# Retention's transposes moved behind the next values, two units of modulation sums moved back, 14 idle products added

## The chip, the cores and the metric

The kernel runs on one core of a Trainium2 chip. The metric is the device time of one execution in microseconds (us); lower is better. TensorE (PE in the profile) multiplies, VectorE (DVE) and ScalarE (ACT) work on elements, GpSimd (POOL) does a few small things, and SyncE (SP) issues nearly all loads, in order, on one queue.

## What is computed

The program is two transformer blocks in float32 on 256 tokens of width 1024. Only the first half of the first block matters here:

```
mod = silu(c) @ w_ada + b_ada                 # 6 x 1024: shift, scale, gate for both halves
h = modulate(rms_norm(x, norm1_g), sh1, sc1)
proj = h @ w_in                               # 14336 columns: retention, attention, two gates
ro = group_norm(retention(rotary(q), rotary(k), v))       # 4 heads, values of 512
ret_out = (silu(rg) * ro) @ w_ret_out
att_out = dilated_attention(3 groups of 4 heads) @ w_att_out
merged = sigmoid(gate_a) * ret_out + sigmoid(gate_b) * att_out
x = x + g1 * (merged @ w_o)
```

`g1` and the modulation of the second half (`sh2`, `sc2`, `g2`) are not needed before `w_o`, though they come from the same vector `c`.

## The kernel before

**Products.** Every float32 product is three products of a rounded type: an operand is split into a high part and a remainder, and `mm3` (L169 to L171) adds high x high, high x low, low x high. Activations are kept transposed (channels on partitions, `h1T`) as such pairs. Weights come in 512 KB loads `raw` (L130, all on SP's queue, a ring of 6); ScalarE rounds a load to `whi` (L145), VectorE subtracts to `wlo` (L148), and both live in rings of 6. A projection of 512 columns is 96 products of 128x256 (or 48 of 128x512 where tokens are the rows).

**Order.** Except where the code says `manual_schedule`, a list scheduler orders the instructions of each engine by its own model of costs; each engine and each queue then works in that order, and an instruction that waits holds up all that stand behind it.

**Start** (ordered by hand). Five steps of `START` each finish the modulation of one or two blocks of 128 channels and use them for the first queries, keys and values. `ada_cols` loads the columns of `w_ada` in pieces (`araw`), VectorE multiplies and sums them row by row (L394, L396), PE adds over partitions (L414, L415, in `rest`), VectorE adds the bias (L417, L419), ScalarE makes `h1T` (L510, L511), PE runs the queries (12 products for one block). `rest(n)` starts with n products of zeros, `busy` (L176), 128x256 in a narrow type. `setup_rest` and constants follow.

**Retention.** For each of 4 heads h: values `a_v` (L601), scores, gate `a_g`, `ret_out` of the two heads before when there are some waiting (`late`), then o (L625 to L627), its mean and variance, the normed rows `y` (L637, VectorE), their transposes (L644, PE) into `r` (L647, ScalarE), times the gate (L648, VectorE), and the split of `r` into `rT` (L289). `ret_out` reads `rT` of two heads. In head 0 three small products of `hot` (L663) and the setup of the second block (L1022 among it) follow.

**Attention.** Three groups of four heads; for each head scores (L701, L702), sum with the bias and maximum (L704, L705, VectorE), `nmx` (L706), exponentials (L707, ScalarE), transposes (L711, PE), product with the values (L716 to L718). Then four projections of the gates (L735, L737), the three groups combined into `att` (L765, VectorE), its transposes (L771), the split into `attT` (L289), `w_att_out`, and `w_o`.

**The rest of the modulations.** Eight units are in the list `side`: the two halves of the gate row `g1` (`ada_row(0, j)`), blocks 0, 2, 4 and 6 of the second half's shift and scale (`ada_block`), the two halves of `g2`. A unit loads 2 MB of `w_ada` in four pieces of 512 KB (for blocks, each piece is two transfers of 256 KB) into buffers of their own, makes eight sums on VectorE (L394 once, L396 seven times) and ends in a product (L415 for blocks, L435 for rows) and a small VectorE operation (L417 and L419, or L436). The buffers `araw` are four during retention (`phase is pr`) and two afterwards. `SIDE[i]` says how many units are pulled after head i (0 to 3), group i - 4 (4 to 6), and the i - 7th gate projection (7 to 10); the scheduler may start what is pulled earlier than that, as buffers allow.

Of the kernel before, what the change touches and what calls it, by code (L numbers as in the profile page):

```python
# [10 lines left out]
F32 = mybir.dt.float32  # L11
# [68 lines left out]
class Kern:  # L80
# [273 lines left out]
    def first(self, done, after):  # L354
# [118 lines left out]
        with tc.manual_schedule():  # L473
# [33 lines left out]
            def activations(kb, sums):  # L507

                tmp = pr.tile([128, 256], F32, name=self.nm("ht"), tag="ht")
                S.activation(tmp, xT[:, kb, :], AF.Identity, scale=mod[:, 8 + kb : 9 + kb], bias=mod[:, kb : kb + 1])  # L510
                S.activation(hT[0][:, kb, :], tmp, AF.Copy)  # L511
                step(sums)
                V.tensor_sub(hT[1][:, kb, :], tmp, hT[0][:, kb, :])
# [15 lines left out]
            for i, g in enumerate(START):  # L529
# [9 lines left out]
                    sums, rest = ada_cols(0, n[0], len(n), 8 - ADA_PE[i + 1])  # L539
                for kb in g:  # L540
                    activations(kb, sums)
                queries(g[0], *qk, (0,))
                last = (g[0], *vs)
                if raws:
# [46 lines left out]
        for h in range(RET_H):  # L591
# [7 lines left out]
                    rotary(qk[:, 2 + j], a_k[j])  # L599
            if h:  # L600
                a_v = self.proj_nat(hT, w_in, [(2048 + h * 512, 512)])  # L601
            q, k = qk[:, h % 2], qk[:, 2 + h % 2]
            v = vcopy(a_v, pr, "v")

# [30 lines left out]
            y = pr.tile([128, 2, 512], F32, name=self.nm("y"), tag="y", bufs=1)  # L635
            for t in range(2):
                V.tensor_scalar(y[:, t], o[t], mv[:, t, 0:1], rs[:, t : t + 1], op0=OP.subtract, op1=OP.mult)  # L637
            r = pr.tile([128, 4, 256], F32, name=self.nm("r"), tag="r", bufs=1)
            for j in range(2):
                p = self.ps(128, 2, 256)  # L640
                for b in range(2):
                    blk = 2 * j + b
                    for t in range(2):
                        PE.transpose(p[:, b, t * 128 : t * 128 + 128], y[:, t, blk * 128 : blk * 128 + 128], self.ident)  # L644
                for b in range(2):
                    ch = h * 4 + 2 * j + b
                    S.activation(r[:, 2 * j + b], p[:, b], AF.Identity, bias=p1[:, 64 + ch : 65 + ch], scale=p1[:, 48 + ch : 49 + ch])  # L647
            V.tensor_mul(r, r, sg)  # L648
            o4 = (h % 2) * 4
            self.split_to(rT[0][:, o4 : o4 + 4], rT[1][:, o4 : o4 + 4], r)  # L650
            if h % 2 == 1:
                late = (rT, (h - 1) * 4)
            if h == 0:
# [14 lines left out]
                self.second_setup()  # L668
            for _ in range(SIDE[h]):
                side.pop(0)()  # L670
        ret_out(*late)
        pr_.close()

# [1322 lines left out]
G1_FREE = 0  # L1996
FREE = 8
REST = 3
SIDE = (0, 0, 0, 2, 0, 2, 1, 1, 0, 1, 1)
BUSY = (0, 7, 13, 0, 9)  # L2000
START = ((0,), (1,), (2, 3), (4, 5), (6, 7))
EARLY = 1
# [136 lines left out]
```

## Time and profile before

| | us |
|---|---|
| runs (three) | 1258.31, 1258.60, 1258.93 |
| median | 1258.6 |
| profiled execution | 1255.0 |
| its span, first to last instruction | 1253.2 |
| PE busy | 1215.2 (97%) |
| DVE busy | 953.8 (76%) |
| ACT busy | 739.3 (59%) |

Times in the rows below are microseconds from the start of the span. In a row of the timeline stand the start, the duration, engine, line of the code, operation, what is written from what, and in brackets how long the engine stood idle before and what ended that. A PE row's duration includes the pipeline's length; the time between two products is read from start to start. The granted clock (PEclk) is 1.00 at 2.4 GHz and 0.50 at 1.2 GHz.

### The profile page before, as it was taken

To read this page: it belongs to the slowest core of one execution; us is meant where nothing else is said; L and a number is where in the kernel's file an instruction comes from. 1 tells how busy PE (TensorE), PEld (TensorE's weight loads), DVE (VectorE), ACT (ScalarE), POOL (GpSimd) and SP (SyncE) were. 2 spreads that over 40 slices of the span, in tenths; PEclk is the share of its full clock that TensorE was granted. 3 is DMA by queue.
4 is the path that set the end of the run, shared out by engine and by line. 5 is a ranking of instruction groups with operands and counts; after the bars stand their busy time and mean duration, and the time that the engine had idled before them with its cause. 6 is when DMAs were issued, how large, how long until landed. Compare 5 with 4: busy or idle time off the path is not lost.

```text
span 1253.2 us, 20725 instructions
## 1 busy us (share of the span) xinstructions
PE 1215.2 (97%) x7675; PEld 1071.7 (86%) x7675; DVE 953.8 (76%) x1650; ACT 739.3 (59%) x1149; POOL 41.6 (3%) x101
## 2 busy tenths in 40 slices
PE   8999999999999999999999998999999999899995
PEld 7878988988989889998898987888879988788884
DVE  6999656574678766555589677999988967798995
ACT  4554444445554655444367663978766665588873
POOL 0010000000000000000010011000000000100000
PEclk9999999999999999999999999999999999999998
DMA  9996554796677656666473432999867342399991
GB/s 312 320 312 209 185 169 152 229 292 187 186 250 250 195 183 197 189 198 187 140 234 109 130 101 73 356 346 360 307 211 227 104 132 84 112 372 343 366 316 55
DMA packets 177170, 271.99 MB, mean 217 GB/s; under 512 B 16363, under 2 KB 109216, under 8 KB 177060
## 3 DMA queue, kind: packets, MB, share of 16 engines
q1 hardware_dynamic: 175252, 265.70, 64.4%
q10 hardware_dynamic: 1296, 3.81, 1.0%
q8 instruction: 62, 1.02, 0.3%
q0 software_dynamic: 512, 1.08, 0.2%
q14 instruction: 48, 0.39, 0.1%
HBM read 268.41 MB, written 2.12 MB: 216 GB/s over the span
## 4 chain that ended last, share of the span: by engine, by line
PE 78%; DVE 10%; DMA 4%; ACT 3%; POOL 2%; issue 2%; SPq 0%; POOLq 0%; DVEq 0%; ACTq 0%
PE ps L171 21%; PE ps L170 21%; PE ps L169 21%; DMA araw<-in_w_ada 2%; DVE wlo L148 2%; DMA raw<-in_w_in 1%; PE ps L1283 1%; PE ps L1264 1%; DVE zc L1196 1%; ACT whi L145 1%; PE ps L1681 1%; DVE ada L396 1%; PE ps L1873 1%; POOL s L285 1%; PE ps L176 1%
## 5 line engine op out<-in xcount | busy, mean ns | idle before, releaser
L145 ACT ACTIVATE whi<-raw 128x1024 fp32r<-128x1024 f32 (+3 forms) x348 | 356.3, 1039 | 262.7 <-PE ps L170 146.5
L148 DVE TENSOR_TENSOR wlo<-raw,whi 128x1024 fp32r<-128x1024 f32 x334 | 398.8, 1205 | 136.5 <-ACT whi L145 134.3
L169 PE MATMUL ps<-h1T,whi 128*128 128x256 f32 x576 | 162.9, 283 | 1.6 <-ACT h1T L511 1.6
L171 PE MATMUL ps<-h1T,wlo 128*128 128x256 f32 x576 | 162.2, 282 | 0.0
L170 PE MATMUL ps<-h1T,whi 128*128 128x256 f32 x576 | 162.0, 281 | 0.0
L148 DVE TENSOR_TENSOR wlo<-far,whi 128x1024 fp32r<-128x1024 f32 x100 | 118.3, 1220 | 7.3 <-ACT whi L145 6.8
L145 ACT ACTIVATE whi<-far 128x1024 fp32r<-128x1024 f32 x100 | 103.6, 1059 | 19.5 <-PE ps L171 18.0
L169 PEld LDWEIGHTS ps<-h1T,whi 128*128 128x128 f32 x576 | 109.0, 189 | 3.4 <-ACT h1T L511 1.7
L170 PEld LDWEIGHTS ps<-h1T,whi 128*128 128x128 f32 x576 | 109.5, 190 | 1.1 <-issue 0.5
L171 PEld LDWEIGHTS ps<-h1T,wlo 128*128 128x128 f32 x576 | 109.1, 190 | 0.2 <-issue 0.2
L169 PE MATMUL ps<-whi,xg 128*128 128x512 f32 x256 | 103.0, 402 | 0.0
L171 PE MATMUL ps<-whi,xg 128*128 128x512 f32 x256 | 100.7, 393 | 0.0
L170 PE MATMUL ps<-wlo,xg 128*128 128x512 f32 x256 | 100.6, 393 | 0.0
L396 DVE SCALAR_TENSOR_TENSOR ada<-araw,silu_c,ada 128x512 f32<-128x512 f32 (+1 forms) x88 | 62.6, 712 | 10.0 <-DMA araw<-in_w_ada 8.1
L169 PE MATMUL ps<-h2T,whi 128*128 128x256 f32 x224 | 62.0, 277 | 0.0
L170 PE MATMUL ps<-h2T,whi 128*128 128x256 f32 x224 | 62.0, 277 | 0.0
L171 PE MATMUL ps<-h2T,wlo 128*128 128x256 f32 x224 | 61.9, 276 | 0.0
L171 PEld LDWEIGHTS ps<-whi,xg 128*128 128x128 f32 x256 | 48.1, 188 | 10.4
L170 PEld LDWEIGHTS ps<-wlo,xg 128*128 128x128 f32 x256 | 48.2, 188 | 9.3 <-DVE wlo L148 0.4
L169 PEld LDWEIGHTS ps<-whi,xg 128*128 128x128 f32 x256 | 48.1, 188 | 8.8
L171 PE MATMUL ps<-whi,ffh 128*128 128x512 f32 x128 | 50.4, 394 | 0.0
L170 PE MATMUL ps<-wlo,ffh 128*128 128x512 f32 x128 | 50.2, 392 | 0.0
(517 smaller groups left out, 2888.3 us busy)
## 6 DMA issues: line engine op xcount, KB each, us to landing
raw<-in_w_in SPq DMA_DIRECT2D x124, 512.0 KB, 4.9
raw<-in_w_ff SPq DMA_DIRECT2D x64, 512.0 KB, 3.7
far<-in_w_gate SPq DMA_DIRECT2D x68, 256.0 KB, 5.2
far<-in_w_up SPq DMA_DIRECT2D x68, 256.0 KB, 5.9
araw<-in_w_ada SPq DMA_DIRECT2D x64, 256.0 KB, 4.9
far<-in_w_down SPq DMA_DIRECT2D x32, 512.0 KB, 5.9
raw<-in_w_down SPq DMA_DIRECT2D x32, 512.0 KB, 7.0
raw<-in_w_gate SPq DMA_DIRECT2D x60, 256.0 KB, 5.5
```

What stands on the lines that cost most here:

```text
L145: self.nc.scalar.activation(hv, raw, AF.Copy)
L148: self.nc.vector.tensor_sub(lv, raw, hv)
L169: mm(out, l[0], r[0], start=first, stop=False)
L170: mm(out, l[0], r[1], start=False, stop=False)
L171: return mm(out, l[1], r[0], start=False, stop=last)
L176: self.nc.tensor.matmul(p, self.idle, self.idle.unsqueeze(1).to_broadcast([128, 2, 128]), start=True, stop=True)
L285: self.nc.gpsimd.tensor_tensor(dst, t, self.mhalf[:, :w] if len(src.shape) == 2 else self.mhalf[:, :w].rearrange("p (a b) -> p a b", a=src ...
L396: V.scalar_tensor_tensor(acc, raws[k], sc[:, k : k + 1], acc, op0=OP.mult, op1=OP.add)
L1196: V.scalar_tensor_tensor(zc[:, b], xp_[:, i, k : k + 256], cw(k), zc[:, b], op0=OP.mult, op1=OP.add)
L1264: PE.matmul(p[:, t], qT[:, j, t * 128 : t * 128 + 128], kT[:, j], start=True, stop=True)
L1283: PE.matmul(p[:, t, j], PTs[j][:, s, t * 128 : t * 128 + 128], v[:, s, h * 64 : h * 64 + 64], start=j == 0 and t == 0 and s == 0, stop=j = ...
L1681: self.nc.tensor.matmul(p[kb // 2][:, kb % 2], xh[i][:, t, kb * 128 : kb * 128 + 128], P[:, t, hf * 256 : hf * 256 + 256], start=t == 0 an ...
```

## The change

Three things. (a) In the first step of the start, 14 idle products are put on PE between the end of `rest` and the queries, into the accumulator that the first query product then starts anew. (b) The part of a retention head from the transposes of `y` to the split into `rT` becomes a function `gated`, and it is called a head later, behind the next head's values; for head 3 it is called right before the last `ret_out`. (c) The table `SIDE` pulls no unit after head 3 any more, and two more units at the gates. Units keep their sequence, so each is pulled later than it was: the two rows of `g1` after group 1 and block 0 after group 2 (before: after head 3, and blocks after groups 1 and 2), blocks 2 and 4 after the first gate projection, block 6 after the second, the rows of `g2` after the third and the fourth.

```diff
@@ start, in the loop over START
                 for kb in g:
                     activations(kb, sums)
+                if i == 0:
+                    self.busy(a_q[0][:, 0].rearrange("p (a b) -> p a b", a=2), 14)
                 queries(g[0], *qk, (0,))
@@ retention, loop over heads
             if h:
                 a_v = self.proj_nat(hT, w_in, [(2048 + h * 512, 512)])
+                waiting()
             q, k = qk[:, h % 2], qk[:, 2 + h % 2]
             v = vcopy(a_v, pr, "v")
...
-            r = pr.tile([128, 4, 256], F32, name=self.nm("r"), tag="r", bufs=1)
-            for j in range(2):
-                p = self.ps(128, 2, 256)
...
-            V.tensor_mul(r, r, sg)
-            o4 = (h % 2) * 4
-            self.split_to(rT[0][:, o4 : o4 + 4], rT[1][:, o4 : o4 + 4], r)
+            def gated(h, y, sg, rT):
+
+                r = pr.tile([128, 4, 256], F32, name=self.nm("r"), tag="r", bufs=1)
+                for j in range(2):
+                    p = self.ps(128, 2, 256)
+                    for b in range(2):
+                        blk = 2 * j + b
+                        for t in range(2):
+                            PE.transpose(p[:, b, t * 128 : t * 128 + 128], y[:, t, blk * 128 : blk * 128 + 128], self.ident)
+                    for b in range(2):
+                        ch = h * 4 + 2 * j + b
+                        S.activation(r[:, 2 * j + b], p[:, b], AF.Identity, bias=p1[:, 64 + ch : 65 + ch], scale=p1[:, 48 + ch : 49 + ch])
+                V.tensor_mul(r, r, sg)
+                o4 = (h % 2) * 4
+                self.split_to(rT[0][:, o4 : o4 + 4], rT[1][:, o4 : o4 + 4], r)
+
+            waiting = lambda a=(h, y, sg, rT): gated(*a)
             if h % 2 == 1:
                 late = (rT, (h - 1) * 4)
...
             for _ in range(SIDE[h]):
                 side.pop(0)()
+        waiting()
         ret_out(*late)
@@ table
-SIDE = (0, 0, 0, 2, 0, 2, 1, 1, 0, 1, 1)
+SIDE = (0, 0, 0, 0, 0, 2, 1, 2, 1, 1, 1)
```

Lines behind the start are numbered differently in the changed kernel: L644 becomes L649, L663 becomes L670, L704 to L706 become L712 to L714, L719 becomes L727, L765 becomes L773.

PE, the end of head 0's part of the values of head 1. `ps_1044` and `ps_1045` are the accumulators of those values, `y` the normed rows of head 0. Before:

```order
536 L171 MATMUL ps_1045<-whi_1066,h1T_108 128x512
537 L169 MATMUL ps_1044<-whi_1066,h1T_107 128x512
538 L170 MATMUL ps_1044<-wlo_1067,h1T_107 128x512
539 L171 MATMUL ps_1044<-whi_1066,h1T_108 128x512
540 L644 MATMUL ps_950<-sq,y_946 128x128
541 L644 MATMUL ps_957<-sq,y_946 128x128
542 L663 MATMUL ps_973<-hot_971,tab 4x384
543 L644 MATMUL ps_950<-sq,y_946 128x128 x3
544 L644 MATMUL ps_957<-sq,y_946 128x128 x3
545 L169 MATMUL ps_1045<-whi_1066,h1T_107 128x512
```

After, where the accumulators are `ps_1040` and `ps_1041`:

```order
595 L170 MATMUL ps_1040<-wlo_1099,h1T_107 128x512
596 L171 MATMUL ps_1040<-whi_1098,h1T_108 128x512
597 L169 MATMUL ps_1041<-whi_1098,h1T_107 128x512
598 L170 MATMUL ps_1041<-wlo_1099,h1T_107 128x512
599 L171 MATMUL ps_1041<-whi_1098,h1T_108 128x512
600 L649 MATMUL ps_1115<-sq,y_960 128x128 x4
601 L649 MATMUL ps_1122<-sq,y_960 128x128 x4
602 L610 MATMUL ps_1135<-qk_775 128x256 x2
```

Before, the transposes stand after 21 of the 48 products; after, behind all 48, and ahead of head 1's scores (L610).

VectorE, group 0 of the attention, around the second head's maximum. `ada` and `araw` belong to the units of `side`, `s`, `mx` and `nmx` to the attention. Before:

```order
287 L396 SCALAR_TENSOR_TENSOR ada_3473<-araw_3477,silu_c,ada_3473 128x512 x2
288 L704 ISA s_2951,mx_2944<-ps_2948,TB_2612 128x256
289 L704 ISA mx_2944 128x1
290 L705 ISA s_2951,mx_2944<-ps_2948,TB_2612 128x128
291 L705 ISA mx_2944 128x1
292 L148 TENSOR_TENSOR wlo_3193<-raw_3190,whi_3192 128x1024
293 L706 TENSOR_SCALAR nmx_2945<-mx_2944 128x2
294 L396 SCALAR_TENSOR_TENSOR ada_3473<-araw_3480,silu_c,ada_3473 128x512 x2
295 L704 ISA s_2971,mx_2944<-ps_2968,TB_2612 128x256
```

After:

```order
267 L396 SCALAR_TENSOR_TENSOR ada_3437<-araw_3440,silu_c,ada_3437 128x512 x2
268 L148 TENSOR_TENSOR wlo_3131<-raw_3128,whi_3130 128x1024
269 L712 ISA s_2919,mx_2912<-ps_2916,TB_2580 128x256
270 L712 ISA mx_2912 128x1
271 L713 ISA s_2919,mx_2912<-ps_2916,TB_2580 128x128
272 L713 ISA mx_2912 128x1
273 L714 TENSOR_SCALAR nmx_2913<-mx_2912 128x2
274 L148 TENSOR_TENSOR wlo_3161<-raw_3158,whi_3160 128x1024
275 L396 SCALAR_TENSOR_TENSOR ada_3437<-araw_3442,silu_c,ada_3437 128x512 x2
276 L712 ISA s_2939,mx_2912<-ps_2936,TB_2580 128x256
```

The sums stand at the same places, but they are those of a row of `g1` where they were those of a block, and `nmx` comes ahead of the split.

VectorE, the end of the gates, around the first split of `attT`. `arow` and `ada` belong to the rows of `g2`, `wlo` to `w_att_out` and `w_o`. Before:

```order
460 L148 TENSOR_TENSOR wlo_4670<-raw_4667,whi_4669 128x1024
461 L148 TENSOR_TENSOR wlo_4700<-raw_4697,whi_4699 128x1024
462 L148 TENSOR_TENSOR wlo_4759<-raw_4756,whi_4758 128x1024
463 L436 TENSOR_TENSOR arow_4504<-arow_4504,ps_4523 1x512
464 L148 TENSOR_TENSOR wlo_4777<-raw_4774,whi_4776 128x1024
465 L289 TENSOR_TENSOR attT_4576<-ps_4577,attT_4575 128x512
466 L289 TENSOR_TENSOR attT_4576<-ps_4584,attT_4575 128x512
```

After:

```order
454 L396 SCALAR_TENSOR_TENSOR ada_4520<-araw_4521,silu_c,ada_4520 128x512
455 L148 TENSOR_TENSOR wlo_4714<-raw_4711,whi_4713 128x1024
456 L148 TENSOR_TENSOR wlo_4773<-raw_4770,whi_4772 128x1024
457 L396 SCALAR_TENSOR_TENSOR ada_4520<-araw_4523,silu_c,ada_4520 128x512 x2
458 L148 TENSOR_TENSOR wlo_4791<-raw_4788,whi_4790 128x1024
459 L396 SCALAR_TENSOR_TENSOR ada_4520<-araw_4525,silu_c,ada_4520 128x512
460 L289 TENSOR_TENSOR attT_4590<-ps_4591,attT_4589 128x512
461 L396 SCALAR_TENSOR_TENSOR ada_4520<-araw_4525,silu_c,ada_4520 128x512
462 L396 SCALAR_TENSOR_TENSOR ada_4520<-araw_4527,silu_c,ada_4520 128x512 x2
463 L148 TENSOR_TENSOR wlo_4809<-raw_4806,whi_4808 128x1024
```

Before, the sums of the last unit are done well ahead of the split; after, five of its eight stand ahead of it and three behind.

## Rows read from the trace of the kernel before

**Rows 1.** The page, busy time of each engine.
```profile
PE 1215.2 (97%) x7675; PEld 1071.7 (86%) x7675; DVE 953.8 (76%) x1650; ACT 739.3 (59%) x1149; POOL 41.6 (3%) x101
```

**Rows 2.** Timeline of PE, the first queries: start, duration, what, idle before.
```profile
15.60 0.48 PE L169 MATMUL ps<-h1T,whi 128*128 128x256 f32 x1 [1.58 <-ACT h1T L511]
...
17.08 0.41 PE L171 MATMUL ps<-h1T,wlo 128*128 128x256 f32 x1
17.29 0.41 PE L169 MATMUL ps<-h1T,whi 128*128 128x256 f32 x1
```

**Rows 3.** Timeline of PE, around the transposes L644 of heads 0, 1, 2.
```profile
81.59 0.39 PE L170 MATMUL ps<-wlo,h1T 128*128 128x512 f32 x1
81.82 0.40 PE L171 MATMUL ps<-whi,h1T 128*128 128x512 f32 x1
82.92 0.44 PE L644 MATMUL ps<-sq,y 128*128 128x128 f32 x2 [0.70 <-DVE y L637]
...
111.87 0.28 PE L170 MATMUL ps<-h1T,whi 128*128 128x256 f32 x1
111.98 0.28 PE L171 MATMUL ps<-h1T,wlo 128*128 128x256 f32 x1
113.41 0.41 PE L644 MATMUL ps<-sq,y 128*128 128x128 f32 x2 [1.15 <-DVE y L637]
...
184.74 0.44 PE L644 MATMUL ps<-sq,y 128*128 128x128 f32 x2 [0.69 <-DVE y L637]
```

**Rows 4.** Stretches: PE, PEld, DVE, ACT, POOL busy, granted clock, DMA share, GB/s.
```profile
16.00:18.00 2.00, 2.00 (x10) 1.94 (x10) 1.86 (x6) 1.02 (x2) 0.00 (x0) 0.50 1.08 382
```

**Rows 5.** Waits of PE in 55 to 240 and 240 to 300 us: total, times, longest.
```profile
PE ps L644 <- DVE y L637: 3.4, 4, 1.2
PE ps L1022 <- DVE gs L1020: 0.4, 1, 0.4
...
PE ps L711 <- ACT s L707: 3.1, 3, 1.4
```

**Rows 6.** Stretches, same columns as rows 4: group 0, and the gates.
```profile
260.00:280.00 20.00, 18.16 (x117) 16.17 (x116) 14.20 (x26) 9.63 (x17) 0.00 (x0) 1.00 0.91 290
367.18:412.59 45.41, 45.41 (x380) 44.25 (x380) 38.13 (x71) 23.68 (x35) 0.97 (x2) 1.00 0.71 231
```

**Rows 7.** Timeline of VectorE, the second step of the start.
```profile
18.92 1.22 DVE L148 TENSOR_TENSOR wlo<-raw,whi 128x1024 fp32r<-128x1024 f32 x1
20.62 0.16 DVE L417 TENSOR_TENSOR mod<-ps,p 128x1 f32<-128x1 f32 x1 [0.48 <-PE ps L415]
```

**Rows 8.** Waits of VectorE in 240 to 300 us: total, times, longest.
```profile
DVE ada L396 <- DMA araw<-in_w_ada: 5.5, 4, 2.0
DVE ada L394 <- DMA araw<-in_w_ada: 3.1, 2, 2.3
```

**Rows 9.** Timeline of VectorE in group 0, two sums before the second head's maximum.
```profile
275.21 1.54 DVE L396 SCALAR_TENSOR_TENSOR ada<-araw,silu_c,ada 128x512 f32<-128x512 f32 x2 [1.61 <-DMA araw<-in_w_ada]
```

**Rows 10.** Timeline of SP's queue and of VectorE: one pair of loads, its first sum.
```profile
343.89 0.88 SPq L130 DMA_DIRECT2D araw<-in_w_ada  x2
...
348.52 1.54 DVE L396 SCALAR_TENSOR_TENSOR ada<-araw,silu_c,ada 128x512 f32<-128x512 f32 x2 [0.94 <-DMA araw<-in_w_ada]
```

**Rows 11.** Timeline of VectorE, the gates.
```profile
367.18 0.16 DVE L417 TENSOR_TENSOR mod<-ps,p 128x2 f32<-128x2 f32 x1 [1.17 <-PE ps L415]
...
367.63 0.47 DVE L394 TENSOR_SCALAR ada<-araw,silu_c 128x512 f32<-128x512 f32 x1
...
388.64 0.74 DVE L396 SCALAR_TENSOR_TENSOR ada<-araw,silu_c,ada 128x512 f32<-128x512 f32 x1
389.31 1.22 DVE L148 TENSOR_TENSOR wlo<-raw,whi 128x1024 fp32r<-128x1024 f32 x1
...
412.59 1.37 DVE L289 TENSOR_TENSOR attT<-ps,attT 128x512 fp32r<-128x512 f32 x2
```

**Rows 12.** Timeline of PE, the first product that reads the split of attT.
```profile
413.32 0.39 PE L170 MATMUL ps<-attT,whi 128*128 128x256 f32 x1 [0.19 <-DVE attT L289]
```

More of the change, by code (lines that the diff above doesn't have):

```diff
@@ L637, in first @@
                 V.tensor_scalar(y[:, t], o[t], mv[:, t, 0:1], rs[:, t : t + 1], op0=OP.subtract, op1=OP.mult)
-            r = pr.tile([128, 4, 256], F32, name=self.nm("r"), tag="r", bufs=1)
-            for j in range(2):
-                p = self.ps(128, 2, 256)
[L641 to L647, printed above, removed]
-            V.tensor_mul(r, r, sg)
-            o4 = (h % 2) * 4
-            self.split_to(rT[0][:, o4 : o4 + 4], rT[1][:, o4 : o4 + 4], r)
+            def gated(h, y, sg, rT):
[13 more added lines that the diff above has]
+            waiting = lambda a=(h, y, sg, rT): gated(*a)
             if h % 2 == 1:
```

## The prediction

> **What bounds the kernel now.** The page comes first [rows 1]: PE is busy 97% of the span and VectorE 76%. With a PE that full, a change can give back only what PE loses: places where it stands still, and places where it runs at half clock. So the next view is the waits of PE, and after it the timeline around each of them.
>
> Four places matter here. (1) In the start phase PE stands 1.58 us before the first queries, and then those run 0.21 us apart (17.08 to 17.29) [rows 2], against 0.11 us for the same shape later (111.87 to 111.98) [rows 3]; the granted clock in 16 to 18 us was 0.50, the 1.2 GHz level [rows 4]. (2) In retention, PE waits four times for the normed rows y at the transposes of L644, 3.4 us in all, and once for L1020, 0.4 us [rows 5]. (3) In the attention's group 0 it waits three times, 3.1 us, at L711 for the exponentials of L707 [rows 5]. (4) From 367 to 413 us it does not wait at all: PE is busy 45.41 of 45.41 us [rows 6]. That last place is where the change puts work.
>
> **The start's 14 idle products.** They stand on PE between the last L415 and the first query product, in a 1.58 us hole. An idle product has the queries' shape, 128x256; at their full pace of 0.11 us [rows 3] fourteen take an estimated 1.5 us and fit. If the clock then stays up, the twelve products of the first step go from 0.21 to 0.11 us each: 1.2 us on PE. But step 1's next modulation needs VectorE: its sums are done when a split L148 starts at 18.92; that ends 1.22 later, at 20.14, and only then comes L417, which started at 20.62 after 0.48 us of waiting for L415 [rows 7]. PE's 1.2 us can therefore move L417 from 20.62 to 20.14, no further: 0.48 us. After that the start hangs on transfers. I take a gain of 0.4, bounds 0.5 and a loss of 0.7 (if the idle products outlast the hole by six slots).
>
> **Retention's transposes behind the next values.** Before, head 0 has 21 products of 128x512 between the last L627 and the first L644, and they run out; PE waits [rows 3]: gaps of 0.70 (head 0, at 82.92), 1.15 (head 1, at 113.41) and 0.69 (head 2, at 184.74). From product to product the loss is a little larger: 111.98 to 113.41 is 1.43, less one slot of 0.11 is 1.32 against a gap of 1.15; 0.17 more for each of three gives 2.54 + 0.51 = 3.05 us. After, all 48 products of the next head's values stand ahead of the transposes: 27 more for head 0 at 0.23 us each (81.59 to 81.82 [rows 3]), 6 us of cover against waits of about one. The waits of these three heads go. Head 3 has no next values; its wait stays. What comes late next is r and its split, a head later than before, but ret_out, which reads them, has the next head's scores and gate ahead of it, except for head 3. The 0.4 us wait of L1022 shrinks, since sixteen sums leave VectorE in this stretch: I add 0.3. Together 3.35, bounds 2.2 (a third of it returns as waits at the products of `hot`, which now stand 17 products apart while their loads share the SP queue with everything else) and 4.0.
>
> **Moving the sums: what leaves.** SIDE pulls two units of 2 MB (one unit: four loads, eight VectorE sums) out of retention, and everything behind them moves back by two units. In group 0 the order of VectorE is what costs: L704 stands behind two sums L396, and these behind a landing: VectorE was idle 5.5 + 3.1 us in 240 to 300 us for such landings [rows 8], 1.61 of it before the pair at 275.21, with the second head's L704 behind it [rows 9]. The units there were blocks, whose loads are two pieces of 256 KB, often with a weight load between them on SP. After, the units there are the two rows of `gate_rows`: one load of 512 KB each, no piece behind a weight load, and the first L706 comes ahead of the split and of the sums. The landing of a pair came 4.63 us after the issue (343.89 to 348.52 [rows 10]); a piece behind a weight load adds the time until that is issued. Three losses of gap + 0.17 make 3.1 + 0.5 = 3.6 us; I count three quarters gone, 2.7, since sums still stand ahead of three of the four tiles. Bounds 0.5 (the rows land as late as the blocks did) and 3.5.
>
> **Moving the sums: what arrives.** Between L417 of the block behind group 2 (367.18) and the first split of attT (412.59) VectorE worked 38.13 of 45.41 us [rows 6, 11], so 7.28 us were free; PE waited 0.19 us for that split already [rows 12], so there is no slack behind it. After, four units of sums start in this stretch where two did. Of the last one three sums stand behind the split. That adds 29 - 16 = 13 sums: eleven L396 at 0.67 us from start to start (388.64 to 389.31), 7.4, two L394 at 0.4 (busy 0.47, and the next starts a little before the end), 0.8, and two more sets of modulations (L417 and L419, 367.18 to 367.63), 0.9: 9.1 us [rows 11]. Were every load there in time, the split would be 9.1 - 7.28 = 1.8 us late, and PE with it.
>
> They are not in time. The loads have two buffers in this phase instead of four; a load is issued when the buffer's second sum is done and must land before the second next chunk's first sum. Between those two points VectorE has, by the order after, some other work. For the third chunk of block 4 that is two sums of the second chunk (1.34), a split L148 (busy 1.22 [rows 11], some 1.15 to the next start), a copy and three ops of eight columns (together an estimated 0.6): 3.1 us. Counted in the same way it is 3.9 and 4.0 for the second and third of block 6, and 4.4 or more elsewhere. Against 4.63 us from issue to landing [rows 10] these fall short by 1.5, 0.7 and 0.6: 2.8 us. The split of attT then comes 1.8 + 2.8 = 4.6 us late. PE gives this up somewhere between L415 of block 4 and the attT products; the wait counts once, whether at L415, at L435 or at attT. Bounds: 1.8 (no landing late), and 1.8 + 9.7 = 11.5 with the blocks' landing waits of group 0 (8.6 us for two units [rows 8]) and 1.1 for the rows.
>
> The Trainium skill (DMA: Bandwidth & Descriptors, Rules for kernel authors) asks to issue a transfer early and wait for it late; the move from four buffers to two does the opposite. The same page's fit (Anatomy of one DMA, 2.0 us and bytes at 436 GB/s) gives 3.2 us for 512 KB as an estimate, by which only 0.1 us would fall short and the total be 1254.0; the row with 4.63 us decides against it.
>
> **Sum.** Gains 0.4 + 3.35 + 2.7 = 6.45, loss 4.6: 1.85 us less. The profiled execution of 1255.0 us (span 1253.2) becomes 1253.1, and the median of 1258.6, which lies 3.6 above it, becomes 1256.7.
>
> **Rivals.** *A, the late sums land in time.* The cost in 367 to 413 us is the bare 1.8: 1258.6 - 6.45 + 1.8 = 1254.0; with the gains at their upper bounds 1252.4. For it: DMA share 0.71 there against 0.91 in 260 to 280 [rows 6]. Against: the pair of 343.89, which still made VectorE wait 0.94 [rows 10]. The page's 3.2 us would make this case. *B, the other side: the loads of blocks 4 and 6 land as in group 0.* Then attT is 11.5 us late: 1258.6 - 6.45 + 11.5 = 1263.6. For it: these blocks were what stalled there, and the weight loads queued on SP behind a late block load go late too. Against: the share of the DMA engines. It ends slower by 0.2% from landing waits of 7.2 us on (9.0 of loss less the 1.8). *C, retention's waits only move:* PE meets them again at the products of `hot`, at L1022 or at r's split; then 1258.6 - 0.4 - 2.7 + 4.6 = 1260.1. Against: the cover of 27 products.
>
> **How the numbers follow.** The forecast, 1256.7, has a chance of 0.42, and by itself a range of 1255 to 1258.5; A 0.30, B 0.13, C 0.15. The range from 1252.0 to 1262.0 takes in C, the forecast, most of A and the lower part of B; about 0.17 lies outside. A measurement tells 0.2%, 2.5 us, from no change. Faster than 1256.1: nearly all of A and over a third of the forecast, 0.43. Slower than 1261.1: most of B and a third of C, 0.18. Within: 0.39.
>
> **What would show it.** Right: no wait at the transposes of y for heads 0 to 2 and one of about 0.8 us for head 3; queries of the first step 0.11 us apart; L711's waits in group 0 under 1 us; and in the gates, where PE had no waits, some 4.6 us of them for VectorE (at L415, L435 or the attT products), with VectorE idle for landings of `araw`. Wrong: the gates' waits under 2 us (A) or over 8 (B); waits of a microsecond each at `hot` or r (C).

## The result, and the profile after

| | before | changed |
|---|---|---|
| median, us | 1258.45 | 1265.94 |
| lowest to highest of four runs | 1257.31 to 1258.93 | 1264.78 to 1268.20 |
| profiled execution | 1255.0 | 1264.87 |
| its span | 1253.2 | 1263.1 |
| mean granted clock | 0.994 | 0.989 |

The changed kernel takes 1.0064 times as long, 95% interval 1.0051 to 1.0077: slower by some 7.5 us, and outside the range that was forecast. A second, identical kernel gave 1266.23 us and 1.0058 (1.0044 to 1.0073).

The page of the changed kernel, busy time by engine. Compare it with [rows 1]: PE is busy 10 us longer for the same 97%, though the change gave it only 14 idle products, so products take longer or wait inside their busy time.

```profile
PE 1225.3 (97%) x7689; PEld 1081.0 (86%) x7689; DVE 954.7 (76%) x1650; ACT 740.6 (59%) x1149; POOL 40.8 (3%) x101
```

**Where PE waits now.** First what PE waits for in 55 to 240 us (retention; total, times, longest). Against [rows 5] three of the four waits for y are gone and the fourth stands, as forecast; a wait for `hot` is new.

```profile
PE ps L670 <- DMA hot<-in_k_hot: 1.0, 1, 1.0
PE ps L649 <- DVE y L640: 0.8, 1, 0.8
```

Group 0's three waits for exponentials [rows 5] do not occur in this execution. Then the gates, where PE had waited 0.2 us in all. The waits of the changed kernel in 366 to 432 us:

```profile
PE ps L170 <- DVE attT L289: 2.3, 1, 2.3
PE ps L169 <- ACT attT L289: 1.1, 1, 1.1
PE ps L169 <- ACT mT L289: 0.7, 1, 0.7
PE ps L435 <- DVE ada L396: 0.4, 1, 0.4
PE ps L415 <- DVE ada L396: 0.2, 1, 0.2
```

Together 4.7 us, about what the prediction allowed for this place. Behind it, in 432 to 520 us, stands what it did not allow for. The first row is of the changed kernel, the second of the kernel before:

```profile
PE ps L830 <- ACT diag L824: 3.5, 2, 3.1
```

```profile
PE ps L822 <- ACT diag L816: 0.7, 2, 0.4
```

**How the lateness travels.** VectorE's timeline of the changed kernel, from the modulation behind group 2 to the first use of `g` (the gate row g1):

```profile
362.48 0.16 DVE L417 TENSOR_TENSOR mod<-ps,p 128x2 f32<-128x2 f32 x1 [1.17 <-PE ps L415]
...
393.35 0.75 DVE L396 SCALAR_TENSOR_TENSOR ada<-araw,silu_c,ada 128x512 f32<-128x512 f32 x1 [0.79 <-DMA araw<-in_w_ada]
...
409.55 1.54 DVE L396 SCALAR_TENSOR_TENSOR ada<-araw,silu_c,ada 128x512 f32<-128x512 f32 x2 [1.39 <-DMA araw<-in_w_ada]
...
412.80 0.69 DVE L289 TENSOR_TENSOR attT<-ps,attT 128x512 fp32r<-128x512 f32 x1
...
415.48 1.54 DVE L396 SCALAR_TENSOR_TENSOR ada<-araw,silu_c,ada 128x512 f32<-128x512 f32 x2 [1.33 <-DMA araw<-in_w_ada]
...
421.36 0.69 DVE L289 TENSOR_TENSOR attT<-ps,attT 128x512 fp32r<-128x512 f32 x1 [0.84 <-ACT attT L289]
...
436.38 0.69 DVE L289 TENSOR_TENSOR mT<-retT,mT 128x512 fp32r<-128x512 f32 x1
...
444.90 0.69 DVE L806 TENSOR_TENSOR gx<-ps,g 128x512 f32<-128x512 f32 x1 [1.69 <-DMA g<-gate_rows]
```

From L417 to the first split of attT it is 412.80 - 362.48 = 50.32 us, where it was 45.41 [rows 11]: 4.91 us more. Before, both splits of attT stood together; now the second one comes 8.56 us after the first. The last split of mT follows at 436.38, and only behind that does ScalarE's queue issue the load of g1, whose memory is that of the pools which close there. Of the changed kernel, the issue:

```profile
437.10 0.34 ACTq L312 DMA_DIRECT2D g<-gate_rows  x1
```

Of the kernel before, the issue, and VectorE's first two uses:

```profile
430.57 0.34 ACTq L312 DMA_DIRECT2D g<-gate_rows  x1
```

```profile
436.95 0.69 DVE L798 TENSOR_TENSOR gx<-ps,g 128x512 f32<-128x512 f32 x1 [0.27 <-DMA g<-gate_rows]
...
439.37 0.69 DVE L798 TENSOR_TENSOR gx<-ps,g 128x512 f32<-128x512 f32 x1 [1.00 <-PE ps L171]
```

Before, then, the load was not what the work behind it waited for: VectorE stood 0.27 us for it, but 1.00 us for PE right after. Now the first use of `g` comes 444.90 - 436.95 = 7.95 us later: the issue 6.53, and the way from issue to first use is 1.42 longer (7.80 against 6.38).

The chain of waits of the changed kernel, in order of time (start, us, what), in the stretch behind it; a few pieces of it. The load is on the chain with 7.71 us, and from there residual, norm and diagonal lead to PE:

```profile
437.10 7.71 DMA g<-gate_rows
...
449.85 0.41 ACT diag L824
...
450.30 3.55 PE ps L830 x16
```

PE's timeline at the same places: of the changed kernel, with the waits in brackets, the first attT products, two pairs of products behind them at two paces, the first product of mT, and L830.

```profile
410.53 0.74 PE L169 MATMUL ps<-attT,whi 128*128 128x256 f32 x4 [1.11 <-ACT attT L289]
413.54 0.58 PE L170 MATMUL ps<-attT,whi 128*128 128x256 f32 x1 [2.28 <-DVE attT L289]
...
414.14 0.41 PE L169 MATMUL ps<-attT,whi 128*128 128x256 f32 x1
414.35 0.41 PE L170 MATMUL ps<-attT,whi 128*128 128x256 f32 x1
...
416.60 0.28 PE L170 MATMUL ps<-attT,whi 128*128 128x256 f32 x1
416.71 0.29 PE L171 MATMUL ps<-attT,wlo 128*128 128x256 f32 x1
...
428.33 0.50 PE L169 MATMUL ps<-whi,mT 128*128 128x512 f32 x1 [0.67 <-ACT mT L289]
...
450.30 0.99 PE L830 MATMUL ps<-diag,x 128*128 128x128 f32 x4 [3.14 <-ACT diag L824]
```

Of the kernel before, the last two of these:

```profile
423.86 0.39 PE L169 MATMUL ps<-whi,mT 128*128 128x512 f32 x1
...
443.16 0.71 PE L822 MATMUL ps<-diag,x 128*128 128x128 f32 x4 [0.39 <-ACT diag L816]
```

The same places side by side show where the 9.9 us between these two spans come from (the medians lie 7.5 apart):

| place | before | changed | changed is later by |
|---|---|---|---|
| L417 behind group 2 | 367.18 | 362.48 | -4.70 |
| first L170 of attT | 413.32 | 413.54 | 0.22 |
| first product of mT | 423.86 | 428.33 | 4.47 |
| load of g1 issued | 430.57 | 437.10 | 6.53 |
| first use of g1 | 436.95 | 444.90 | 7.95 |
| L822 / L830 begins | 443.16 | 450.30 | 7.14 |
| end of the span | 1253.2 | 1263.1 | 9.9 |

Up to the end of the attention the change is a gain of 4.7 us in this execution (in that of e12, the identical kernel, L417 is at 365.58, a gain of 1.6). In the next 90 us all of it goes, and 7.1 us more.

**And the clock.** Windows of the changed kernel (stretch, length, busy time of PE, PEld, DVE, ACT, POOL, granted clock, DMA share, GB/s), ahead of L830's first product and behind it:

```profile
445.00:450.00 5.00, 2.16 (x10) 1.44 (x8) 3.87 (x6) 1.60 (x5) 1.16 (x2) 1.00 0.99 392
450.00:455.00 5.00, 4.70 (x22) 4.47 (x23) 1.11 (x4) 3.00 (x8) 0.00 (x0) 0.66 0.13 51
```

PE stands still for more than half of 445 to 450 us, and then runs at a mean of 0.66, between the two levels 2.4 GHz (1.00) and 1.2 GHz (0.50). It is the same at attT: behind the 2.28 us wait a product takes 0.21 us (414.14 to 414.35), later 0.11 (416.60 to 416.71). The two stretches cost about 14 x 0.10 = 1.4 us at attT and 0.34 x 4.70 = 1.6 us behind L830. The kernel before has 1.00 in all of 400 to 480 us. Once more, in 1076 to 1082 us, the changed kernel's clock is 0.72 with PE busy 4.97 us, some 0.28 x 4.97 = 1.4 us; but such a fall between 1065 and 1090 us is in the traces of e2 and e9 too, which take less time than the kernel before, and not in that of e3, which has the table, so it is not put down to the table.

### The profile page after: what moved, and what is told of

It reads as the page before. It is cut to its first block, busy times and chain, and to the rows that moved or that the text cites. A ratio compares the mean times of both kernels' runs of the same rounds, so it can differ in the third digit from the quotient of the medians.

```text
span 1263.1 us, 20750 instructions
## 1 busy us (share of the span) xinstructions
PE 1225.3 (97%) x7689; PEld 1081.0 (86%) x7689; DVE 954.7 (76%) x1650; ACT 740.6 (59%) x1149; POOL 40.8 (3%) x101
## 4 chain that ended last, share of the span: by engine, by line
PE 54%; DVE 6%; ACT 2%; POOL 1%; issue 1%; DMA 1%; POOLq 0%; ACTq 0%; DVEq 0%
PE ps L171 15%; PE ps L169 14%; PE ps L170 14%; PE ps L1291 1%; PE ps L1272 1%; DVE zc L1204 1%; PE ps L1881 1%; PE ps L1689 1%; DMA g<-gate_rows 1%; PE ps L1412 1%; PE ps L1516 1%; PE ps L1851 1%; PE ps L1282 1%; ACT whi L145 1%; PE ps L1320 0%
## 5 line engine op out<-in xcount | busy, mean ns | idle before, releaser
L170 PE MATMUL ps<-h1T,whi 128*128 128x256 f32 x576 | 162.8, 283 | 0.1
L170 PEld LDWEIGHTS ps<-h1T,whi 128*128 128x128 f32 x576 | 109.7, 190 | 1.9 <-issue 1.0
L170 PE MATMUL ps<-wlo,xg 128*128 128x512 f32 x256 | 100.6, 393 | 0.0
L396 DVE SCALAR_TENSOR_TENSOR ada<-araw,silu_c,ada 128x512 f32<-128x512 f32 (+1 forms) x88 | 62.7, 713 | 11.5 <-DMA araw<-in_w_ada 9.9
L170 PE MATMUL ps<-h2T,whi 128*128 128x256 f32 x224 | 62.0, 277 | 0.0
L171 PEld LDWEIGHTS ps<-whi,xg 128*128 128x128 f32 x256 | 48.1, 188 | 10.5
L170 PEld LDWEIGHTS ps<-wlo,xg 128*128 128x128 f32 x256 | 48.2, 188 | 9.3 <-DVE wlo L148 0.4
L170 PE MATMUL ps<-wlo,ffh 128*128 128x512 f32 x128 | 50.2, 392 | 0.0
```

The source lines that it names most:

```text
L170: mm(out, l[0], r[1], start=False, stop=False)
L171: return mm(out, l[1], r[0], start=False, stop=last)
L396: V.scalar_tensor_tensor(acc, raws[k], sc[:, k : k + 1], acc, op0=OP.mult, op1=OP.add)
```

## The experiments

Each is compared with the kernel before run beside it. The ratio is to that, with its 95% interval.

### The three parts apart

**e1_idle_only**: the kernel before, with the 14 idle products.

```diff
+                if i == 0:
+                    self.busy(a_q[0][:, 0].rearrange("p (a b) -> p a b", a=2), 14)
```

> Before with the 14 idle products alone. Theory (the cost lies in the moved sums): the trace of the changed kernel has the start's end 0.57 us later, with the low clock moved from 16-20 to 20-34 us, so no gain: +0.0 to +0.9 us against before. Rival (the idle products gain by themselves what was predicted, and the 0.57 comes from something later): -0.4 us.

Measured: 1258.02 us, 1.0005 (0.9987 to 1.0022). The idle products neither gain nor cost anything that shows.

**e2_deferred_only**: the kernel before, with `gated` called a head later.

```diff
+                waiting()
...
+            waiting = lambda a=(h, y, sg, rT): gated(*a)
...
+        waiting()
         ret_out(*late)
```

> Before with the transposes moved behind the next values alone, SIDE as before. Theory: the waits at the transposes of heads 0 to 2 go (3.05 us from product to product), a wait of 1 us for the loads of hot comes: -1.5 to -3 us. Rival (moving the transposes also leaves long stretches of 128x256 products at 0.1178 us apart where before had 0.1133, some 600 products x 0.0045 = 2.7 us): -0.5 to +1 us, and the stretches 95 to 109 and 219 to 271 us show 0.1178.

Measured: 1254.06 us, 0.9975 (0.9961 to 0.9989), so 3.7 us less (the interval is 1.4 to 4.9); more than was expected here, and the 3.35 us of the prediction's term lie within the interval.

**e3_side_only**: the kernel before, with the new table.

```diff
-SIDE = (0, 0, 0, 2, 0, 2, 1, 1, 0, 1, 1)
+SIDE = (0, 0, 0, 0, 0, 2, 1, 2, 1, 1, 1)
```

> Before with the new SIDE alone. Theory (the loss is the late sums): group 0's waits go (3.6 us), 366 to 470 us loses 11 to 12 us against before (stall at attT near 5, at L830 near 3 to 4, the moved products 1.7): +6 to +9 us. Rival (the loss needs the moved transposes as well): below +4 us.

Measured: 1267.44 us, 1.0073 (1.0049 to 1.0097), 9.65 us more. The whole loss sits in this one line. What PE waits for in 360 to 480 us is what it waits for in the changed kernel, and in the same places:

```profile
PE ps L822 <- ACT diag L816: 3.3, 2, 3.0
PE ps L170 <- DVE attT L289: 3.2, 1, 3.2
```

**e4_idle_and_deferred**: the changed kernel, with the old table.

```diff
-SIDE = (0, 0, 0, 0, 0, 2, 1, 2, 1, 1, 1)
+SIDE = (0, 0, 0, 2, 0, 2, 1, 1, 0, 1, 1)
```

> The changed kernel with the SIDE of before. Theory: what the first two give together, -1 to -3 us against before, 8 to 11 us below the changed kernel; no wait at attT over 0.3 us. Rival (paces): -0.5 to +1.5 us.

Measured: 1252.73 us, 0.9961 (0.9946 to 0.9977), 5.1 us less. This beats the kernel before. The parts do not add up exactly: -5.1 and +9.65 make 4.5, the pair measures 7.5 to 8.5. The intervals, about 2 us wide to either side for the one and 3 for the other, do not exclude a plain sum, so no interaction is claimed.

### What in the table's change costs

**e5_three_buffers**: the changed kernel, a third buffer for `araw` behind retention.

```diff
-... bufs=ADA_BUFS if phase is pr else 2)
+... bufs=ADA_BUFS if phase is pr else 3)
```

> The changed kernel with three buffers for the loads of the sums (araw) in the phase of attention and gates instead of two. Theory (VectorE has too much to do in the gates, and landings add to it): the landing waits of araw in 362 to 416 us (3.5 us) go, the sums' work stays, the split of attT comes 2 to 3 us late instead of 4.9: 3 to 5 us below the changed kernel, +2 to +5 us against before. Rival (the landings alone are the cause): the whole loss of the gates goes, -2 to -4 us against before. Rival (the work alone): within 1 us of the changed kernel.

Measured: 1258.19 us, 1.0000 (0.9984 to 1.0015): as fast as the kernel before, where 2 to 5 us above it were expected. That is some 8 us below the changed kernel, but not all of the table's loss: e4, with the old table and two buffers, is at 0.9961, some 5 us lower still. The third buffer also led the scheduler to another order, with all sums of the last unit ahead of the split of attT. PE's waits in 366 to 432 us:

```profile
PE ps L435 <- DVE ada L396: 2.5, 1, 2.5
PE ps L415 <- DVE ada L396: 1.4, 1, 1.4
```

There is none at attT, and L830 waits 0.7. So the third buffer matters, but buffers and order changed together; how much belongs to which stays open.

**e7_short_sums**: the changed kernel with only two of the eight sums for the rows of g2; all loads stay.

```diff
-            acc, sums, _ = ada_acc([(base, 512)], 512)
+            acc, sums, _ = ada_acc([(base, 512)], 512, 2 if which else 8)
```

> The changed kernel with only two of eight sums for each of the two rows of g2 (so g2 is wrong); all loads stay. VectorE has 12 sums, 8 us, less in the gates. Theory (VectorE's work there is the larger part): no wait over 0.5 us at attT, 8 to 12 us below the changed kernel, -4 to 0 us against before. Rival (loads and queue order are the cause): less than 4 us below the changed kernel.

Measured: 1254.79 us, 0.9973 (0.9962 to 0.9984): 11 us below the changed kernel. The loads are all there, twelve sums of 0.67 us (8 us) are not, and with them go VectorE's waits for landings of `araw` (3.5 us in 362 to 425 us of the changed kernel, none here). What PE waits for in 366 to 432 us:

```profile
PE ps L415 <- DVE ada L396: 0.2, 1, 0.2
PE ps L170 <- DVE attT L289: 0.2, 1, 0.2
```

So the traffic by itself does not make PE late; VectorE's sums, together with their waits for landings, do, and 8 us of sums cost more than 8 us. The run does not part the sums' work from their waits.

**e9_one_unit**: the changed kernel with one unit back after head 3, and one less at the first gate projection.

```diff
-SIDE = (0, 0, 0, 0, 0, 2, 1, 2, 1, 1, 1)
+SIDE = (0, 0, 0, 1, 0, 2, 1, 1, 1, 1, 1)
```

> The changed kernel with SIDE = (0, 0, 0, 1, 0, 2, 1, 1, 1, 1, 1): one unit moved back instead of two. Theory (a threshold: VectorE has 7.3 us free ahead of the split of attT, a unit costs 5.2 us with its small operations): the split comes no later than in before (45.4 us behind L417 of the block behind group 2), PE's waits in 366 to 432 us under 1 us: -3 to -6 us against before, 11 us or more below the changed kernel. Rival (each moved unit costs the same): halfway, +0 to +3 us.

Measured: 1253.25 us, 0.9963 (0.9947 to 0.9978). Half of the units moved costs nothing of the loss. VectorE's anchor and split, which are 46.97 us apart (45.41 before, 50.32 in the changed kernel):

```profile
364.86 0.16 DVE L417 TENSOR_TENSOR mod<-ps,p 128x2 f32<-128x2 f32 x1 [1.17 <-PE ps L415]
...
411.83 1.27 DVE L289 TENSOR_TENSOR attT<-ps,attT 128x512 fp32r<-128x512 f32 x2
```

With 1.56 us more between them PE waits 0.9 at attT and 0.7 at L830, and both splits of attT again stand together (x2). So the cost does not grow evenly with the units moved. Two things differ between one unit and two: whether VectorE's free 7.28 us take the added sums in, as the expectation had it, and the scheduler's order, by which with two units three sums of the last unit, and its L435 on PE, stand between the two splits of attT. All traces side by side, in us: the second split behind the first, then the stretch of PE's way in four pieces (VectorE's L417 behind group 2 to the first L170 of attT, from there to the first product of mT, to the first product of the diagonal, L822 to L830 by kernel, and to the end of the span):

| kernel | second split | to attT | to mT | to the diagonal | to the end | ratio to before |
|---|---|---|---|---|---|---|
| before | together (one row, x2) | 46.14 | 10.54 | 19.30 | 810.0 | |
| e1, e2, e4, e11 | together | 46.1 to 46.4 | 10.5 to 10.6 | 19.3 | 809.7 to 811.2 | 0.9961 to 1.0005 |
| e8 | together | 46.35 | 10.94 | 19.13 | 810.0 | 0.9948 |
| e9 | together | 47.70 | 10.55 | 19.29 | 811.1 | 0.9963 |
| e7 | together | 48.61 | 10.54 | 19.29 | 809.8 | 0.9973 |
| e5 | 416.47 - 415.38 = 1.09 | 55.03 | 10.54 | 19.34 | 809.8 | 1.0000 |
| e10 | 421.98 - 413.14 = 8.84 | 51.46 | 15.08 | 19.52 | 811.0 | 1.0020 |
| changed | 421.36 - 412.80 = 8.56 | 51.06 | 14.79 | 21.97 | 812.8 | 1.0064 |
| changed again (e12) | 426.62 - 416.88 = 9.74 | 52.04 | 15.98 | 21.60 | 811.1 | 1.0058 |
| e3 | 427.54 - 418.70 = 8.84 | 52.83 | 15.09 | 21.81 | 811.3 | 1.0073 |
| e6 | 425.23 - 415.20 = 10.03 | 52.05 | 16.29 | 24.29 | 812.7 | 1.0080 |

Every kernel whose splits are torn apart, by 8 us or more, is slower than before, and no other is, clear of noise. e5 tells most: PE's first L170 comes 8.9 us later behind L417 than before, later than in any other kernel, and yet the next two pieces take 10.54 and 19.34 us, as before. There the late split costs its lateness once. What comes on top, 4.3 to 5.8 us up to mT in every kernel with torn splits and 2.3 to 5.0 up to the diagonal in those of them that load g1, comes with the tearing. This is read across kernels, and e5 has a third buffer as well; no run keeps the splits together and changes nothing else.

### How the lateness gets to L830

**e6_g1_other_place**: the changed kernel, g1's load in another place of the pool and on GpSimd's queue.

```diff
-        g1 = self.row(pm, gd[0:1], D, "g1")
         x1 = self.new_x("x1")
         h2T = ...
+        g1 = self.row(pm, gd[0:1], D, "g1", eng=G)
```

> The changed kernel with the tile g1 allocated behind h2T in its pool and loaded from GpSimd's queue instead of ScalarE's, where the load stood behind the last split of mT (issue at 437.1 us, used at 444.9, VectorE idle 1.7 us for it, PE 3.1 us at L830). Theory (the late load of g1 is a second loss beside the split of attT): PE's wait at L830 falls under 1 us: 2.5 to 4 us below the changed kernel, +3.5 to +5 against before. Rival (L830 waits for VectorE's splits of w_ff1, which end at 443.2, in any case): within 1 us of the changed kernel.

Measured: 1267.99 us, 1.0080 (1.0061 to 1.0099). A miss: the load waits for the same split of mT. GpSimd's row, the time of this load from issue to landing (the last number), and PE's wait in 432 to 520 us:

```profile
441.49 0.56 POOL L312 DMA_DIRECT2D g<-gate_rows  x1 [16.34 <-DVE mT L289]
```

```profile
g<-gate_rows POOLq DMA_DIRECT2D x1, 512.0 KB, 9.5
```

```profile
PE ps L830 <- ACT diag L824: 5.8, 2, 5.5
```

It is issued 4.39 us later than in the changed kernel (441.49 against 437.10), but the second split of attT, too, comes 3.87 later in this execution (425.23 against 421.36), so only some 0.5 us of that are the load's own; and it takes 9.5 us to land, where the changed kernel's took 7.71. PE's wait at L830 grows by 2.4 us (3.1 to 5.5). L830 begins 456.51 - 451.0 = 5.5 us behind the landing here, and 450.30 - 444.81 = 5.5 in the changed kernel: in both, PE follows the load.

**e10_gate_from_x**: the changed kernel; the residual takes its gate from x, which lies in memory already, and g1 is not loaded.

```diff
-        g1 = self.row(pm, gd[0:1], D, "g1")
...
-            residual(x1, x, acc, g1, 0, 0, ms[0])
+            residual(x1, x, acc, x[:, 0], 0, 0, ms[0])
... (and so the three other calls of residual)
```

> The changed kernel with the first residual's gate read from the tile x in place of g1 (so the result is wrong), and no load of g1. Theory (the load of g1, which cannot start before the last split of mT, is a second loss): PE's wait at L830 falls from 3.1 us to 1.5 or less, since VectorE still ends its splits of w_ff1 at about 443 us: 1.5 to 3 us below the changed kernel, +4.5 to +6 against before. Rival (the wait is the splits alone): within 1 us of the changed kernel.

Measured: 1260.09 us, 1.0020 (1.0005 to 1.0034): 6 us below the changed kernel, where 1.5 to 3 were expected, and still 2.3 above the kernel before. VectorE does not wait for `g`, PE waits 0.69 at L829, and the clock behind it stays up:

```profile
448.48 1.27 PE L829 MATMUL ps<-diag,x 128*128 128x128 f32 x9 [0.69 <-ACT diag L823]
```

```profile
450.00:455.00 5.00, 5.00 (x26) 4.15 (x26) 3.61 (x8) 2.61 (x7) 0.00 (x0) 1.00 0.02 5
```

The wait of 3.14 less 0.69 is 2.45, the clock's part 1.6: 4.1 of the 6 us are found in the trace, the rest is not. That g1's load hands the lateness on is shown: from the first product of mT to the diagonal it is 19.52 us, nearly what it was before (19.30), with the splits as far apart as in e3. It is not the whole of the loss, since PE's waits ahead of mT are still there.

### Another table, and the noise

**e8_rows_in_group1**: e4 with the rows of g1 pulled after group 0, three buffers and e6's load.

```diff
-SIDE = (0, 0, 0, 0, 0, 2, 1, 2, 1, 1, 1)
+SIDE = (0, 0, 0, 0, 2, 2, 1, 1, 0, 1, 1)
```

> Idle products and moved transposes of the change, SIDE = (0, 0, 0, 0, 2, 2, 1, 1, 0, 1, 1): the rows of g1 pulled after group 0, nothing moved into the gates; three buffers, g1 loaded as in the run before. Theory (sums are harmless where VectorE has room, 300 to 360 us): gates as in before, group 0's waits as in the changed kernel (under 0.5 us): -5 to -8 us against before. Rival (any unit later than retention costs): above -3 us.

Measured: 1251.88 us, 0.9948 (0.9930 to 0.9966): the best kernel of the study, below both. Against e4 (0.9961) the difference is within the intervals.

**e11_rows_group1_plain**: the same table in the changed kernel, with its two buffers and its g1.

> The changed kernel with SIDE = (0, 0, 0, 0, 2, 2, 1, 1, 0, 1, 1) and nothing else: the two rows of g1 pulled after group 0, two buffers, g1 loaded as before. Theory: as the run with three buffers and this table, -5 to -7 us against before: where the sums stand decides, not the buffers. Rival (the three buffers gave it): above -4 us.

Measured: 1255.05 us, 0.9984 (0.9970 to 0.9997): 2.7 us below the kernel before, where e8 is 5.7 below. Both have the idle products and the later transposes, which gave e4 its 5.1, so by itself this table gains nothing over the old one. Where e11 loses against e8, VectorE's waits for landings ahead of L396 in 240 to 366 us tell, first of e11, then of e8:

```profile
DVE ada L396 <- DMA araw<-in_w_ada: 13.3, 9, 3.4
```

```profile
DVE ada L396 <- DMA araw<-in_w_ada: 2.5, 5, 0.7
```

In e11 PE waits 4.9 us in 240 to 366 us for exponentials, in e8 not at all. So with the table held, group 0's waits go with the landings. Buffers and g1's load were not separated here, though e5, with three buffers and g1's load as it was, has no such wait either.

**e12_changed_again**: the changed kernel once more, nothing edited.

> The changed kernel once more. Theory (the 128x256 products run at one of two paces, 0.1133 or 0.1178 us, which an execution falls into at small products, not by its program): the stretches at 0.1178 differ from the first trace's (95 to 109, 144 to 178, 194 to 208, 219 to 271, 282 to 322 us) in some places: +6 to +10 us against before. Rival (the pace belongs to the program): the same stretches.

Measured: 1266.23 us, 1.0058 (1.0044 to 1.0073). PE waits at the same places (at attT 1.1 and 2.0 us, at mT 0.7; at L830 3.1 us, 2 times). In group 0, however, one wait of 2.0 us for exponentials is there, which the first trace did not have, and the clock is low at attT for longer (0.62 in 415 to 420 us, 0.69 in 420 to 425) and not behind L830 (1.00 in 455 to 460), though PE waited 2.8 us there.

## Why the prediction was wrong, step by step

**The start** (0.4 us less). The queries did run at full pace, as the rows of the changed kernel say (16.75 to 16.86 is 0.11 us, [rows 2] had 0.21), and the first query came at 15.26 us. The second L417 came at 19.72, earlier than the 20.14 that the term took for its bound. But L415 there waits for VectorE's sums:

```profile
16.75 0.28 PE L169 MATMUL ps<-h1T,whi 128*128 128x256 f32 x1
16.86 0.28 PE L170 MATMUL ps<-h1T,whi 128*128 128x256 f32 x1
...
18.72 0.38 PE L415 MATMUL ps<-sq,ada 128*128 128x1 f32 x2 [0.57 <-DVE ada L396]
```

and the granted clock in 20 to 34 us is 0.76, where it was 0.88. In this execution the saving went into a wait and into the clock: the start's last L417 comes at 52.53, where it came at 51.96. That is not fixed: in e12 the clock in 20 to 34 us is 1.00 and that L417 comes at 51.37. e1 measures nothing clear of noise, within the stated bounds.

**Retention** (3.35 less). Right in mechanism and size. The waits for y fall from 3.4 us [rows 5] to 0.8, head 3's; a wait of 0.96 at `hot` takes a part back, as the lower bound had it; alone, the edit is worth 3.7 us (e2, 1.4 to 4.9).

**Group 0** (2.7 less). In the first trace all three waits are gone, a gain of 3.1 and the gaps' rest, but that was luck of one execution. The six traces with the new table and two buffers have 0, 2.0 (e12), 1.7 (e3), 3.2 (e6), 3.0 (e7) and 1.1 us (e10) of such waits, 1.8 on the mean; the four with the old table have 3.1, 3.8 (e1), 1.8 (e2) and 2.3 (e4), 2.8 on the mean. So the table's own part is about 1 us, and not clear of the spread. The term was mis-sized, taken too near its upper bound.

**The late sums** (4.6 more at the split of attT). Right in size: 4.91. Its parts came out near. VectorE worked 46.61 us ahead of the split, 8.5 more than before, where 9.1 were counted; the landings that the term took as 2.8 late show as 0.79 + 1.39 = 2.18 us ahead of the split, and 1.33 behind it; and 1.5 us of other short waits stand ahead of it, which the term did not have. The Trainium skill (DMA: Bandwidth & Descriptors, Anatomy of one DMA), by whose fit a 512 KB load lands in an estimated 3.2 us, made them land all but in time; it gives that fit for transfers that GpSimd issues, and these stand on SP's queue. The median from issue to landing of the eight 512 KB loads in 366 to 432 us is 4.1 us, so the row that was preferred to it, 4.63 [rows 10], was nearer.

```profile
araw<-in_w_ada SPq DMA_DIRECT2D x8, 512.0 KB, 4.1
```

**The step that failed** is the sentence after that sum: PE gives this up somewhere between L415 of block 4 and the attT products, and the wait counts once. It counts once where both splits of attT stay together (e5); in the changed kernel it does not. The prediction said a little earlier that three sums of the last unit stand behind the split, and gave them no price. There are two splits of attT; the order listed ahead of the prediction shows both together before (465 and 466), but afterwards one only (460) ahead of the three sums: they stand between the two. The term's 4.9 us stands in the table above as -4.70 to 0.22, and then come three more items which the prediction had at nothing:

- From 0.22 to 4.47, up to the first product of mT. The three sums stand ahead of the second split (421.36), and PE's pair of L435 and half of attT's transposes stand there with them, 418.78 to 420.45, 1.7 us of work that lay ahead of the split before. PE also runs at half pace behind its wait (1.4 us) and waits 0.67 for mT.
- From 4.47 to 7.14, up to L830. The load of g1 is issued right behind the last split of mT, which comes later by 2.1 us more than mT's first product does, and from issue to first use it is 1.4 us longer (why, stays open). Before, VectorE had waited 1.00 us for PE behind the first use; 0.8 us of this slack went, and 2.1 + 1.4 - 0.8 are the 2.7 at L830. e10, without the load, and e6, with a slower one, show this link from either side.
- From 7.14 to 9.9: the low clock behind L830, 1.6 us, which goes when the wait goes (e10) but does not come with every such wait (e12), and the one at 1076 us, 1.4, which other kernels have without the table.

What would the sum have been? Against the kernel before, the four pieces of the long table add up to 4.92 + 4.25 + 2.67 + 2.76 = 14.6 us in the first trace of the changed kernel, and to 14.7 in the second. Of this, 1.6 are products that only moved here: two blocks' L415, eight products each, in 0.82 us (361.49 to 362.31 for one set), which stand in for two rows' products in retention. So the table costs some 13 us, less what it gains in group 0, about 1 (e3, without the other two parts, measured 9.65, interval 6.2 to 12.2). With the 5.1 that the other two parts give (e4) the kernel ends some 7 to 8 us slower; 7.5 and 8.5 were measured. Of the prediction's terms, then, the gates cost some 9 us more than it allowed, group 0 gave 1 to 2 us less, and the start's 0.4 did not show. This is worked out afterwards, and single pieces vary by a microsecond between executions.

**The rivals.** B had the right sign, and a price of 11.5 that is close to the loss, but for another reason: it had landings 9.7 us late, and they were 2.2. That is the right number by the wrong mechanism; e7, which leaves every load in place, speaks against traffic as the cause, though it takes the waits for landings out too. A fell; C, that retention's waits only move, fell with e2.

## What to carry to other kernels

When work is moved to a place where the bound engine has no wait, look in the new order at what has come to stand between two halves of one step: half of the move cost nothing (e9), the whole of it tore the splits of attT apart, and what a late but whole split cost (e5) was its lateness alone. Then follow the lateness past the first wait to the next transfer that can be issued only behind it: here a load into memory that is handed over from closing buffers, with 1 us to spare before. Allow, for each wait of a few microseconds on PE, for what a lower granted clock may take behind it, from a row of the same trace (1.4 and 1.6 us here). And read a term off several executions before you count it: group 0's waits went from 0 to 3.2 us with the same table.

## What the runs showed of the hardware

Products of 128x256 that follow each other without a wait, at a granted clock of 1.00, run at one of two paces: 0.1133 or 0.1178 us from start to start. A pace holds for tens to hundreds of products. In the traces of the two kernels and of e12 and e8 it changes where products of another shape stand between; the one change seen within a run of 128x256 products, at the same place in three of the four traces, comes behind two short breaks (in the changed kernel 217.02 to 217.35 and 218.84 to 219.03, with 0.113 us between products before and 0.118 after). It is not fixed by the program: the identical kernel has the one pace in a place in one execution and the other in another. Three products further on, in the changed kernel (0.36 us) and in e12 (0.34 us), at the same place of the same program:

```profile
284.96 0.28 PE L169 MATMUL ps<-h1T,whi 128*128 128x256 f32 x1
...
285.32 0.28 PE L169 MATMUL ps<-h1T,whi 128*128 128x256 f32 x1
```

```profile
287.85 0.28 PE L169 MATMUL ps<-h1T,whi 128*128 128x256 f32 x1
...
288.19 0.28 PE L169 MATMUL ps<-h1T,whi 128*128 128x256 f32 x1
```

Up to 470 us the kernel before has 656 products at the slower pace and the changed kernel 1411; 755 x 0.0045 = 3.4 us, at most, of the 9.9 us between these two executions (where PE waits for VectorE anyway, the pace costs nothing). It does not explain the medians: e8 has 1534 of them and is the fastest kernel. What makes the pace change stays open. It is a reason not to read a few microseconds between two single traces as an effect of an edit.
